# Attention's value products with hi and lo probabilities in one moving operand, part sums added by accumulating loads

## The chip, the cores and the metric

The kernel runs on one core of one Trainium2 chip. The metric is the device time of one execution in microseconds, as the median of several runs; lower is better. A core has TensorE (matmuls, with its weight loads), VectorE, ScalarE, GpSimd, and SyncE, whose queue issues nearly all DMAs of this kernel.

## What is computed

One layer over 1024 tokens of width 1024, in float32:

```python
h = rmsnorm(x, g_mix_pre)
proj = h @ w_in                      # q, k, v and forget logits of 8 heads, q, k, v of 8 more
y_fox = forgetting_attention(...)    # softmax(q.k/8 + c[t] - c[s]) v, causal; c = cumsum(log sigmoid(f))
y_chk = chunked_relpos_attention(...)  # softmax(q.k/8 + bias) v, own and 8 previous chunks of 64
x = x + rmsnorm(concat(rmsnorm(y_fox), rmsnorm(y_chk)) @ w_out)
x = x + rmsnorm(memory_cross_attention(rmsnorm(x), rmsnorm(mem)))   # 4 heads, 256 memory tokens
x = x + rmsnorm(square(relu(rmsnorm(x) @ w_ff1)) @ w_ff2)           # hidden 4096
```

Heads have 64 columns. A tolerance close to float32 is wanted, so the kernel splits each factor into a hi and a lo part in the rounded matmul format (F32R) and multiplies hi·hi, hi·lo and lo·hi.

## The kernel before

**Stages.** First the inputs are normalised and the values of the first eight heads ("f") are projected (`value_part`, `values_out`). Then comes one long attention phase (`attention_phase`), in which the q, k and later v projections of 8 pairs of heads, the scores, the transposes of the probabilities, the value products, the keys and values of the memory and the first half of the output projection are interleaved. After it follow the second half of the output projection, the cross attention, and the two matrices of the MLP, each in an order written out by hand.

**Who sets the order in attention.** The order is not written out; a planner in the kernel makes it while the program is recorded. `Flow` keeps a clock of its own. Generators (`value_steps`, `turn_steps`, `score_steps`, `side_steps`, `rstd_steps`, `filler_steps`, in this order of preference) each offer the next step of TensorE with a cost in microseconds and a condition; the first whose condition holds is recorded. Work of other engines is put into lists for VectorE "V", ScalarE "S", GpSimd "G" and the DMA queue "D" with a cost (`flow.put`, `flow.chain`, `flow.load`) and is recorded when the clock reaches it. `Tokens` count free buffers of each kind. On the chip each engine then runs its own list in order; a step that comes sooner or later than planned doesn't change the order, it makes an engine wait.

**Value products.** For a head and a group of two query blocks of 128, `turn_steps` transposes the probabilities of two key blocks into one bank of PSUM (four squares of 128; at an edge of the mask one of them is dead and left out, and the slots are turned so that it is the first or the last). ScalarE copies the bank to a hi tile `ph` (L582), VectorE makes the lo tile `pl` (L579). `value_steps` then multiplies (L613): the stationary operand is a tile of 128 keys by 128 columns, 64 of the values' hi part and 64 of their lo part. It is loaded for each matmul. Four matmuls make a step: (first key block, ph), (second, ph), (second, pl), (first, pl), each over the one or two live query blocks, all summed in one tile `pv`. Its partitions 0 to 63 hold hi values times (hi + lo) probabilities, 64 to 127 the lo values'. When a group's steps are through, ScalarE copies `pv` to `ot` (L622) and two DMAs store the two halves of partitions to DRAM tensors `od…h` and `od…l` (L628).

**Head outputs.** `Outputs.one` later loads both parts of a block of 128 rows by 512 tokens (L929), adds them (L920; GpSimd for the first half of the heads, VectorE for the second), splits the sum into hi and lo (L921, L922), squares it (L924) and sums the squares (L899). `rstd_steps` sums them over partitions by matmuls `ssh` (L942), and a GpSimd power (L950) gives the factor that `mix_steps` applies to the output projection.

**Gates.** `side_steps` transposes the log-forget gates by eight matmuls `ftr` (L401) when the planner's clock has passed 10; ScalarE copies them out, a VectorE scan (L409) sums them along the tokens, and the sums go by way of DRAM (`cd`) to the bias tiles of the "f" heads. Its three tiles `ea`, `la`, `ua` use three of the four `klo` buffers, which otherwise hold the lo part of the keys.

**Buffers.** The large tiles come from a pool `u4` of 34 buffers of 4 KB a partition. PSUM has two banks each of four kinds: `mm` (projections), `s` (scores), `tr` (transposes) and `pv`.

Of the kernel before, what the change touches and what calls it, by code (L numbers as in the profile page):

```python
# [14 lines left out]
F32 = mybir.dt.float32  # L15
F32R = mybir.dt.float32r
# [6 lines left out]
P = 128  # L23
# [112 lines left out]
def build(ctx, tc, nc, out, t):  # L136
# [16 lines left out]
    def u4(name, shape, dt=F32R):  # L153

        return up.tile(list(shape), dt, tag="u4", bufs=34, name=name)
# [44 lines left out]
    od = [[[dr.tile([P, HT], F32, name=f"od{k}_{h}{m}") for m in "hl"] for h in range(2)] for k in range(KC)]  # L200
# [18 lines left out]
    def bias_rows(part):  # L219

        if part == 0:
# [14 lines left out]
            dict(s=2, tr=2, pv=2, mm=2, sp=5, p=2, klo=4, bias=2, raw=2, w=2, ot=3, u4=6,  # L236
# [139 lines left out]
    def forget_gates():  # L376

        z, e, l, u = [p1.tile([P, TB, 8], F32, tag="fg", bufs=4, name=f"f{n}") for n in "zelu"]
        ea, la, ua = [p1.tile([8, S], F32, tag="klo", bufs=4, name=f"f{n}a") for n in "elu"]
# [27 lines left out]
        def scan():  # L407
            vec.memset(ua, 0.0)
            vec.tensor_tensor_scan(la, ea, ua, 0.0, op0=ALU.add, op1=ALU.add)  # L409
# [146 lines left out]
    def turn_steps():  # L556
        for n, a, g in units:
            for c, (kbs, slots, dead) in enumerate(key_steps(n, g)):
# [8 lines left out]
                ph = p1.tile([P, 4, P], F32R, tag="ph", bufs=2, name=f"ph{nm}")  # L567
                pl = p1.tile([P, 4, P], F32R, tag="pl", bufs=2, name=f"pl{nm}")
# [15 lines left out]
                trs[n, a, g, c] = ph, pl  # L584
# [3 lines left out]
    def value_steps():  # L588
        landed = [all_of(("od", k), 32) for k in range(2)]
        for n, a, g in units:  # L590
# [4 lines left out]
            for c, (kbs, slots, dead) in enumerate(steps):  # L595
                yield (0.48, lambda: there(("t", n, a, g, c), ("v", n, 0), ("v", n, 1))
                       and (c or free["pv"].ready() and free["ot"].ready()))
                if c == 0:
                    free["pv"].take()
                    pv = mm_tile([P, 2, P], f"pv{n}{a}{g}", "pv")  # L600
                ph, pl = trs.pop((n, a, g, c))
                full = 1 if dead == [0] else 0
                todo = [(full, ph), (1 - full, ph), (1 - full, pl), (full, pl)]
                for m, (half, x) in enumerate(todo):
# [3 lines left out]
                    else:  # L608
# [4 lines left out]
                    nc.tensor.matmul(pv[:, q0:q0 + k1 - k0, :], v, x[:, k0:k1, :], start=c == 0 and m == 0,  # L613
                                     stop=c + 1 == len(steps) and m == 3, skip_group_check=True)
                free["p"].give(flow.end)

            def leave(pv=pv, kind=kind, nm=f"{n}{a}{g}", a=a, kcol=kcol, g=g, step=1 if kind == "f" else -1):
                box = {}

                def copy():  # L620
                    box["t"] = p1.tile([P, 2, P], F32, tag="ot", bufs=3, name=f"ot{nm}")
                    nc.scalar.activation(box["t"][:, :, ::step], pv, AF.Copy)  # L622

                def store(at):
                    free["pv"].give(at)
                    done = all_of(("ot", nm), 2, lambda end: (free["ot"].give(end), landed["fc".index(kind)](end)))
                    for m in range(2):
                        flow.load(at, lambda m=m: nc.sync.dma_start(  # L628
                            od[kcol][g // 2][m][a * 64:a * 64 + 64, (g % 2) * 256:(g % 2) * 256 + 256],
# [1558 lines left out]
```

## Time and profile before

| | |
|---|---|
| runs of the kernel before | 1488.75 us median of 3 (1487.15 to 1489.96) |
| the profiled execution | 1486.78 us, of which the span of the core's instructions is 1485.0 |
| TensorE busy | 1462.4 us, 98% |
| VectorE, ScalarE, GpSimd busy | 927.7, 796.4, 378.1 us |
| DMA | 239.5 MB, 161 GB/s on average |

The busy shares say which engine is full over the whole span; a share of a stretch of 100 us says it for a stage. A row of a group gives the number of instructions, the sum and the mean of their durations and the idle time ahead of them. A row of the timeline gives start and duration of instructions that follow each other, and in brackets the idle time of the engine ahead of them and what ended it. Durations of neighbouring matmuls overlap, so that the distance between starts is the better measure of what one costs. Times in the timeline count from the start of the span. The stretches list, for each window, busy time of TensorE, its weight loads, VectorE, ScalarE and GpSimd, each with its number of instructions, then the granted TensorE clock (1.00 is full speed), the share of the DMA engines and their GB/s.

### The profile page before, as it was taken

To read this page: it belongs to the slowest core of one execution; us is meant where nothing else is said; L and a number is where in the kernel's file an instruction comes from. 1 tells how busy PE (TensorE), PEld (TensorE's weight loads), DVE (VectorE), ACT (ScalarE), POOL (GpSimd) and SP (SyncE) were. 2 spreads that over 40 slices of the span, in tenths; PEclk is the share of its full clock that TensorE was granted. 3 is DMA by queue.
4 is the path that set the end of the run, shared out by engine and by line. 5 is a ranking of instruction groups with operands and counts; after the bars stand their busy time and mean duration, and the time that the engine had idled before them with its cause. 6 is when DMAs were issued, how large, how long until landed. Compare 5 with 4: busy or idle time off the path is not lost. (4 is left out here: it accounts for less than half of the span.)

```text
span 1485.0 us, 21433 instructions
## 1 busy us (share of the span) xinstructions
PE 1462.4 (98%) x7564; PEld 1245.2 (84%) x7564; DVE 927.7 (62%) x1599; ACT 796.4 (54%) x1426; POOL 378.1 (25%) x464
## 2 busy tenths in 40 slices
PE   8899999999999999999999999999999999999998
PEld 7788888888889988888888887888888888888886
DVE  4857666466465654974374587675555665656577
ACT  7647666576566663563354454545555553443542
POOL 1334344335244310421031423432233000000021
PEclk9999999999999999999999999999999999999999
DMA  8033323424225568451241446764444685435475
GB/s 327 29 94 108 93 65 98 148 69 137 83 73 153 186 244 305 153 202 57 91 164 58 140 159 228 240 241 151 154 156 171 243 345 184 142 137 203 176 249 198
DMA packets 95355, 239.54 MB, mean 161 GB/s; under 512 B 11896, under 2 KB 20224, under 8 KB 95248
## 3 DMA queue, kind: packets, MB, share of 16 engines
q1 hardware_dynamic: 95248, 238.18, 46.8%
q8 instruction: 59, 0.97, 0.3%
q14 instruction: 48, 0.39, 0.1%
HBM read 170.45 MB, written 59.30 MB: 155 GB/s over the span
## 5 line engine op out<-in xcount | busy, mean ns | idle before, releaser
L579 DVE TENSOR_TENSOR pl<-ptr,ph 128x512 fp32r<-128x512 f32 (+1 forms) x152 | 92.4, 616 | 63.5 <-ACT ph L582 63.0
L582 ACT ACTIVATE ph<-ptr 128x512 fp32r<-128x512 f32 (+1 forms) x152 | 79.8, 540 | 48.5 <-PE ptr L573 45.9
L1912 ACT ACTIVATE whif<-ra 128x1024 fp32r<-128x1024 f32 x37 | 39.3, 1062 | 122.3 <-PE fy L175 62.6
L1914 DVE TENSOR_TENSOR wlof<-ra,whif 128x1024 fp32r<-128x1024 f32 x37 | 45.3, 1225 | 91.2 <-ACT whif L1912 91.1
L2028 POOL TENSOR_SCALAR rf<-sf 128x1 f32<-128x1 f32 x8 | 8.3, 1032 | 325.4 <-ACT jf L2013 325.1
L176 PE MATMUL fx<-vhif,wlof 128*128 128x512 f32 x168 | 65.4, 389 | 0.0
L175 PE MATMUL fx<-vlof,whif 128*128 128x512 f32 x168 | 65.4, 389 | 0.0
L174 PE MATMUL fx<-vhif,whif 128*128 128x512 f32 x168 | 65.4, 389 | 0.0
L613 PE MATMUL pv<-pl,vs 128*128 128x256 f32 (+1 forms) x304 | 64.6, 294 | 0.2 <-DVE pl L579 0.2
L613 PEld LDWEIGHTS pv<-ph,vs 128*128 128x128 f32 x304 | 53.1, 189 | 7.3
L613 PE MATMUL pv<-ph,vs 128*128 128x256 f32 (+1 forms) x304 | 58.1, 272 | 0.0
L1802 POOL TENSOR_TENSOR sc<-wf,wf 128x512 f32<-128x512 f32 x14 | 21.3, 1522 | 143.5 <-DMA wf<-in_w_ff 113.2
L174 PE MATMUL k<-hT_hi,whik 128*128 128x512 f32 x128 | 52.6, 411 | 0.0
L174 PE MATMUL q<-hT_hi,whiq 128*128 128x512 f32 x128 | 51.1, 399 | 1.3 <-DVE qs L703 1.3
L174 PE MATMUL mq<-h2T_hi,whimq 128*128 128x512 f32 x128 | 51.6, 403 | 0.0
L174 PE MATMUL yw<-whiwo,yT_hi 128*128 128x512 f32 x128 | 50.6, 396 | 0.4 <-ACT yt L1065 0.4
L174 PE MATMUL ym<-whimo,oT_hi 128*128 128x512 f32 x128 | 50.3, 394 | 0.1
L176 PE MATMUL k<-hT_hi,wlok 128*128 128x512 f32 x128 | 50.3, 393 | 0.0
L175 PE MATMUL k<-hT_lo,whik 128*128 128x512 f32 x128 | 50.3, 393 | 0.0
L176 PE MATMUL q<-hT_hi,wloq 128*128 128x512 f32 x128 | 50.1, 392 | 0.1
L175 PE MATMUL q<-hT_lo,whiq 128*128 128x512 f32 x128 | 50.1, 392 | 0.0
L175 PE MATMUL mq<-h2T_lo,whimq 128*128 128x512 f32 x128 | 50.0, 391 | 0.0
(597 smaller groups left out, 4979.7 us busy)
## 6 DMA issues: line engine op xcount, KB each, us to landing
ra<-gd SPq DMA_DIRECT2D x56, 512.0 KB, 3.5
wg<-in_w_ff SPq DMA_DIRECT2D x56, 512.0 KB, 4.9
wf<-in_w_ff SPq DMA_DIRECT2D x38, 512.0 KB, 3.9
gd<-s SPq DMA_DIRECT2D x48, 256.0 KB, 2.1
wrawmq<-in_w_mq SPq DMA_DIRECT2D x16, 512.0 KB, 3.8
wrawmo<-in_w_mo SPq DMA_DIRECT2D x16, 512.0 KB, 3.7
gd<-u SPq DMA_DIRECT2D x32, 256.0 KB, 2.1
gd<-g SPq DMA_DIRECT2D x25, 256.0 KB, 2.2
```

Of the source, the lines that this page charges most:

```text
L174: nc.tensor.matmul(ps, lh, rh, start=start, stop=False, skip_group_check=more)
L175: nc.tensor.matmul(ps, lh, rl, start=False, stop=False, skip_group_check=more)
L176: nc.tensor.matmul(ps, ll, rh, start=False, stop=stop, skip_group_check=more)
L579: flow.put("V", at, 0.56 if dead else 0.7, lambda: nc.vector.tensor_sub(pl[:, live, :], tr[:, live, :], f(ph[:, live, :])), done)
L582: flow.put("S", flow.end, 0.49 if dead else 0.6, lambda ph=ph, tr=tr, live=live: nc.scalar.activation(ph[:, live, :], tr[:, live, :], AF.C ...
L613: nc.tensor.matmul(pv[:, q0:q0 + k1 - k0, :], v, x[:, k0:k1, :], start=c == 0 and m == 0, stop=c + 1 == len(steps) and m == 3, skip_group_ ...
L1802: eng.tensor_sub(sc[:, k1], r0[:, k0], r1[:, k0])
L1912: nc.scalar.activation(ah, ra, AF.Copy)
L1914: nc.vector.tensor_sub(al, ra, f(ah))
L2028: nc.gpsimd.tensor_scalar(r, ssf[b][:, 0:1], ssf[b][:, 1:2], EPS, op0=ALU.add, op1=ALU.add)
```

## The change

Four things are edited together.

1. **One moving operand.** `ph` and `pl` become the halves of one tile `both`. A step is two matmuls instead of four; each sends the hi and the lo probabilities of one key block through one load of the values, as up to 512 columns. `pv` now has separate sums for hi and for lo probabilities, 512 columns, a whole bank.
2. **Three parts, added by loads.** `ot` and its copy are twice as wide. Two DMAs store three parts: hi·hi and hi·lo (partitions 0 to 63, both sums) and lo·hi (64 to 127, the first sum); lo·lo, which was summed before, is dropped. `Outputs.one` loads part 0 from SyncE's queue and adds parts 1 and 2 by two DMAs on GpSimd's queue that accumulate into the loaded tile, one after the other. The adds on GpSimd and VectorE go, and so do the tiles `oil`.
3. **Gates.** The sum of gates uses the two `bias` buffers instead of three of `klo`; its scan takes a minimum with its own input in place of an add of zeros, so that the memset goes. The transposes of the gates wait until the planner's clock has passed 13 instead of 10.
4. **Buffers.** `u4` has 32 buffers instead of 34 (the planner starts with 8 free tokens instead of 6), the room goes to the wider `ot` and to 4096 bytes of scratch for DMAs from GpSimd (256 before); the tile `rt` moves to the tag `ot`. The planner's costs follow: a value step 0.35 or 0.46 instead of 0.48, the copy 0.6 instead of 0.4, an accumulate 0.9 on GpSimd and 4.5 until it has landed.

```diff
-        return up.tile(list(shape), dt, tag="u4", bufs=34, name=name)
+        return up.tile(list(shape), dt, tag="u4", bufs=32, name=name)
...
-        ea, la, ua = [p1.tile([8, S], F32, tag="klo", bufs=4, name=f"f{n}a") for n in "elu"]
+        ea, la = [p1.tile([8, S], F32, tag="bias", bufs=2, name=f"f{n}a") for n in "el"]
...
-            vec.memset(ua, 0.0)
-            vec.tensor_tensor_scan(la, ea, ua, 0.0, op0=ALU.add, op1=ALU.add)
+            vec.tensor_tensor_scan(la, ea, ea, 0.0, op0=ALU.add, op1=ALU.min)
...
-                todo = [(full, ph), (1 - full, ph), (1 - full, pl), (full, pl)]
-                for m, (half, x) in enumerate(todo):
+                for m, half in enumerate((full, 1 - full)):
...
-                    nc.tensor.matmul(pv[:, q0:q0 + k1 - k0, :], v, x[:, k0:k1, :], start=c == 0 and m == 0,
-                                     stop=c + 1 == len(steps) and m == 3, skip_group_check=True)
+                    nc.tensor.matmul(pv[:, :, q0 * P:(q0 + k1 - k0) * P], v, x[:, :, k0:k1, :].rearrange("p m k q -> p m (k q)"),
+                                     start=c == 0 and m == 0, stop=c + 1 == len(steps) and m == 1, skip_group_check=True)
...
-        yield 0.87, lambda: flow.now > 10.0 and free["tr"].ready(2)
+        yield 0.87, lambda: flow.now > 13.0 and free["tr"].ready(2)
...
-                            (eng, add_cost, lambda: adder.tensor_add(o, o, low)),
...
-                    for m, x in enumerate((o, low)):
-                        flow.load(flow.now, lambda x=x, kc=kc, m=m: nc.sync.dma_start(x, od[kc][th][m]), here, 3.0)
+                    def add(at, m=1, o=o, src=od[kc][th], loaded=loaded):
+                        if m == 3:
+                            return loaded(at)
+                        flow.put("G", at, 0.9, lambda: nc.gpsimd.dma_start(o, src[m], accum_op=ALU.add),
+                                 lambda end: add(end + 4.5, m + 1, o, src, loaded), 1)
+
+                    flow.load(flow.now, lambda o=o, src=od[kc][th]: nc.sync.dma_start(o, src[0]), add, 3.0)
```

Three places of the program's order. The first is on TensorE at the start of attention: `k` and `q` are the projections of the first pair of heads, `q_1…` (here q_1_943, then q_1_915) the second half of the queries, `ftr` the gates' transposes. Before:

```order
L176 MATMUL k_0_890<-hT_hi_200,wlok_804 128x512
L174 MATMUL k_0_890<-hT_hi_201,whik_803 128x512
L175 MATMUL k_0_890<-hT_lo_205,whik_803 128x512
L176 MATMUL k_0_890<-hT_hi_201,wlok_804 128x512
L401 MATMUL ftr_925<-ident,fe 8x128 x4
L401 MATMUL ftr_930<-ident,fe 8x128 x4
L174 MATMUL k_0_890<-hT_hi_201,whik_803 128x512
L175 MATMUL k_0_890<-hT_lo_205,whik_803 128x512
L176 MATMUL k_0_890<-hT_hi_201,wlok_804 128x512
L174 MATMUL q_1_943<-hT_hi_206,whiq_798 128x512
```

And now, at the same place:

```order
L176 MATMUL k_0_873<-hT_hi_185,wlok_787 128x512
L174 MATMUL q_1_915<-hT_hi_190,whiq_781 128x512
L175 MATMUL q_1_915<-hT_lo_194,whiq_781 128x512
L176 MATMUL q_1_915<-hT_hi_190,wloq_782 128x512
L174 MATMUL q_1_915<-hT_hi_190,whiq_781 128x512
L175 MATMUL q_1_915<-hT_lo_194,whiq_781 128x512
L176 MATMUL q_1_915<-hT_hi_190,wloq_782 128x512
L174 MATMUL q_1_915<-hT_hi_191,whiq_781 128x512
L175 MATMUL q_1_915<-hT_lo_195,whiq_781 128x512
L176 MATMUL q_1_915<-hT_hi_191,wloq_782 128x512
L401 MATMUL ftr_932<-ident,fe 8x128 x4
L401 MATMUL ftr_937<-ident,fe 8x128 x4
```

The transposes have moved behind the last k matmuls and behind nine of the q half.

The second place is on TensorE as well, in the first head's first group: two full value steps and one with a dead square (`vs` are values, a row with "x2" two equal instructions). Before:

```order
L613 MATMUL pv_1198<-ph_1163,vs_0_190 128x256 x2
L613 MATMUL pv_1198<-pl_1164,vs_0_190 128x256 x2
...
L613 MATMUL pv_1198<-ph_1232,vs_3_193 128x256
L613 MATMUL pv_1198<-ph_1232,vs_3_193 128x128
L613 MATMUL pv_1198<-pl_1233,vs_3_193 128x128
L613 MATMUL pv_1198<-pl_1233,vs_3_193 128x256
```

Now:

```order
L611 MATMUL pv_1178<-p_1145,vs_0_174 128x512 x2
L611 MATMUL pv_1178<-p_1152,vs_1_175 128x512 x2
...
L611 MATMUL pv_1178<-p_1207,vs_3_177 128x512
L611 MATMUL pv_1178<-p_1207,vs_3_177 128x2x128
```

Two matmuls with 512 columns stand for four with 256, and 512 and twice 128 for 256, 128, 128 and 256.

The third is GpSimd's queue at the second and third group of head outputs (`oin` are the loaded tiles, `rs` the power behind the sum of squares `ssh`). Before, the only rows of `oin` there are the two adds of the second group:

```order
L920 TENSOR_TENSOR oin_6620<-oin_6620,oil_6622 128x512 x2
L920 TENSOR_TENSOR oin_6621<-oin_6621,oil_6623 128x512 x2
```

Now the accumulates of the second group end (first four rows), and those of the third and fourth follow:

```order
L924 DMA oin_6120<-od_1_88 128x512
L924 DMA oin_6120<-od_1_90 128x512
L924 DMA oin_6121<-od_1_92 128x512
L924 DMA oin_6121<-od_1_94 128x512
L924 DMA oin_6300<-od_0_95 128x512
L924 DMA oin_6300<-od_0_97 128x512
L924 DMA oin_6301<-od_0_99 128x512
L924 DMA oin_6301<-od_0_101 128x512
L948 TENSOR_TENSOR rs_6361<-rs_6361,mhalf 128x4
L924 DMA oin_6300<-od_0_95 128x512
L924 DMA oin_6300<-od_0_97 128x512
L924 DMA oin_6301<-od_0_99 128x512
```

The second accumulates of the third group stand behind the power `rs`, which waits for `ssh`. On TensorE 57 output matmuls (`yw`) stood between the end of the memory's keys (`mk`) and `ssh` of the second group before, and 87 now.

More of the change, by code (lines that the diff above doesn't have):

```diff
@@ L198, in build @@
     rall = const.tile([P, TB], F32, name="rall")
[L200 removed]
+    od = [[dr.tile([3, P, HT], F32, name=f"od{k}_{h}") for h in range(2)] for k in range(KC)]
     yd = [dr.tile([P, D], F32, name=f"yd{b}") for b in range(TB)]
@@ L883, in pump @@
                 self.left.pop(0)
-                for _ in range(9):
+                for _ in range(7):
                     free["u4"].take()
@@ L892, in one @@
             os = [u4(f"oin{th}{g}{i}", (P, 2, HT), F32) for i in range(2)]
-            ol = [u4(f"oil{th}{g}{i}", (P, 2, HT), F32) for i in range(2)]
-            eng, add_cost, adder = ("G", 1.45, nc.gpsimd) if g == 0 else ("V", 0.7, nc.vector)
             parts[th, g] = yh, yl, sq
@@ L903, in done @@
                     seen["sq", th, g] = end
-                    for _ in range(4):
+                    for _ in range(2):
                         free["u4"].give(end)
```

39 lines of the change are left out of this document (19 added, 20 removed).

## The prediction

> **What bounds the kernel now.** I read the page first, for the busy shares, then the list of what TensorE waited for, then the stretches.
>
> ```profile
> PE 1462.4 (98%) x7564; PEld 1245.2 (84%) x7564; DVE 927.7 (62%) x1599; ACT 796.4 (54%) x1426; POOL 378.1 (25%) x464
> PE v L174 <- ACT hT_hi L1380: 6.1, 2, 5.2
> PE ftr L401 <- DVE vs L1437: 3.4, 1, 3.4
> PE tr_h3T L1114 <- DVE ym L1010: 1.5, 1, 1.5
> PE q L174 <- DVE qs L703: 1.3, 1, 1.3
> 300.00:400.00 100.00, 99.91 (x611) 88.77 (x610) 61.28 (x182) 65.80 (x144) 41.67 (x55) 1.00 0.31 93
> ```
>
> TensorE is busy for 1462 of 1485 us, and in the attention phase for 99.9 of 100 us. No single wait is over 6 us. So time can only come from TensorE's own stream of instructions, and it is lost wherever that stream starts to wait. Since matmuls overlap, the mean time of one says little; what counts is the distance from one start to the next, read from the timeline.
>
> **Part 1: the value matmuls (L613).** This is how many there are, by shape, and what a step of them takes:
>
> ```profile
> L613 PE MATMUL pv<-pl,vs 128*128 128x256 f32 x224 | 55.6, 300 | 0.0
> L613 PE MATMUL pv<-pl,vs 128*128 128x128 f32 x80 | 22.2, 277 | 0.2 <-DVE pl L579 0.2
> 129.96 0.40 PE L176 MATMUL q<-hT_hi,wloq 128*128 128x512 f32 x1
> 130.20 0.28 PE L500 MATMUL sf1g<-kd,qs 128*128 128x256 f32 x1
> 130.32 0.28 PE L501 MATMUL sf1g<-kl,qs 128*128 128x256 f32 x1
> 130.44 0.40 PE L613 MATMUL pv<-ph,vs 128*128 128x256 f32 x2
> 130.67 0.40 PE L613 MATMUL pv<-pl,vs 128*128 128x256 f32 x2
> 130.91 0.28 PE L500 MATMUL sf1g<-kd,qs 128*128 128x256 f32 x1
> ...
> 132.28 0.34 PE L613 MATMUL pv<-ph,vs 128*128 128x256 f32 x2
> 132.46 0.44 PE L613 MATMUL pv<-pl,vs 128*128 128x128 f32 x2
> 132.74 0.39 PE L174 MATMUL q<-hT_hi,whiq 128*128 128x512 f32 x1
> ...
> 301.13 0.33 PE L500 MATMUL sc0g<-kd,qs 128*128 128x384 f32 x1
> 301.30 0.34 PE L501 MATMUL sc0g<-kl,qs 128*128 128x384 f32 x1
> ```
>
> Half of the matmuls are listed (pl; the ph half is the same), so 304 of each kind and 608 in all, four to a step: 152 steps. A step at an edge of the mask has one short half (128 columns), and there are 80 of those; 72 are full. A matmul with 512 columns takes 0.23 to 0.24 us to the next start (129.96 to 130.20), one with 384 takes 0.17 (301.13 to 301.30), one with 256 takes 0.12: the cost goes by columns. A full step takes 130.91 - 130.44 = 0.47 us, which is four times 0.12. A step with a short half takes 132.74 - 132.28 = 0.46 us, though it has 768 columns instead of 1024, which at this rate would be 0.35. It is therefore not bound by its columns but by something that counts matmuls: each brings its own weight load, and 0.46 / 4 = 0.115 us each is what four loads would need one after the other, since a 128-column matmul is too short to hide the next load.
>
> The change sends hi and lo probabilities through one weight load. A full step becomes two matmuls of 512: 2 x 0.23 = 0.46 us, against 0.47: 72 x 0.01 = 0.7 us. A short step becomes 512 and 256 columns: 0.23 + 0.12 = 0.35 us, against 0.46, and both are long enough to hide a load of 0.115: 80 x 0.11 = 8.8 us. Together **9.5 us less**, all of it on TensorE's path. No row shows a moving operand of two separate runs. If its second run cost as much as a matmul of its own, nothing would be gained; at the other end, full steps that follow transposes may save a little more, and I put the most at 12.5. I take 9.5, since columns set the cost in all rows whose loads are hidden.
>
> Each step's copy out of PSUM (L622) doubles to 128x512, on ScalarE:
>
> ```profile
> L622 ACT ACTIVATE ot<-pv x64: 362/384/387, 111.0 to 515.7; 128x256 f32<-128x256 f32 x64
> L924 ACT ACTIVATE oin<-oin x12: 613/621/637, 349.4 to 544.9; 128x512 f32<-128x512 f32 x12
> L579 DVE TENSOR_TENSOR pl<-ptr,ph 128x512 fp32r<-128x512 f32 (+1 forms) x152 | 92.4, 616 | 63.5 <-ACT ph L582 63.0
> wg<-in_w_ff SPq DMA_DIRECT2D x56, 512.0 KB, 4.9
> ```
>
> That is 64 x (0.62 - 0.38) = 15 us more over 400 us in which ScalarE is 66% busy; it becomes 70%, and I cost it at nothing. If the cover were gone it would be at most those 15 us. The first matmul of a step now needs the lo half as well as the hi half; the planner waited for both anyway, so this costs nothing, and uncovered it would be up to one VectorE split (0.62 us) for a step. Two u4 buffers fewer, of which the planner now counts two more as free, I cost at nothing: in the program's order a u4 buffer is written again no sooner than 69 instructions after its last use (94 before), some 7 us at 9 instructions to a microsecond, and the weights of the last stage (4.9 us to land) are fetched four steps of 24 matmuls ahead, 22 us. Uncovered it would be a few microseconds for each late load.
>
> **Part 2: the gate sums, later.** At the start of attention, rows of TensorE and then of the engines that it waits for:
>
> ```profile
> 67.01 0.39 PE L176 MATMUL k<-hT_hi,wlok 128*128 128x512 f32 x1
> 70.77 1.86 PE L401 MATMUL ftr<-ident,fe 128*8 128x128 f32 x8 [3.37 <-DVE vs L1437]
> 72.28 0.77 PE L174 MATMUL k<-hT_hi,whik 128*128 128x512 f32 x1
> 75.17 0.47 PE L174 MATMUL q<-hT_hi,whiq 128*128 128x512 f32 x1 [1.26 <-DVE qs L703]
> 72.20 1.39 DVE L228 COPY rrow<-rrow 8x511 f32<-8x511 f32 x1
> 73.61 1.41 DVE L703 SCALAR_TENSOR_TENSOR qs<-q,qs 64x512 fp32r<-64x512 f32 x2
> 76.91 2.28 DVE L409 TENSOR_TENSOR_SCAN fla<-fea,fua 8x1024 f32<-8x1024 f32 x1
> 86.08 0.29 POOL L462 TENSOR_SCALAR_AFFINE_SELECT biasf<-biasf 128x128 f32<-128x128 f32 x1 [10.13 <-DMA biasf<-cd]
> 92.25 0.39 PE L500 MATMUL sf0g<-kd,qs 128*128 128x512 f32 x1
> 70.70:72.20 1.50, 1.43 (x7) 0.88 (x8) 1.47 (x6) 1.49 (x3) 1.46 (x2) 0.50 0.00 0
> 74.00:76.00 2.00, 0.83 (x4) 0.74 (x5) 1.78 (x4) 1.24 (x3) 1.95 (x2) 1.00 0.73 246
> ```
>
> The second query half (q, from 75.17) can't start before VectorE has emptied the bank of the first, at 75.0. In the meantime the kernel before does the eight gate transposes (ftr) and three k matmuls for free. In the changed order three k matmuls and then nine of the q half stand ahead of ftr. VectorE's rows up to L703 are the same, so q still starts at 75.15; TensorE now runs out of k matmuls at about 67.9 (67.01 and four times 0.23) and idles in one piece of 7.2 us, and ftr is paid after it: 8 x 0.11 = 0.9 us. The granted clock fell to 0.50 after the idle piece of 3.4 us, and was 1.00 again some 3 us after work resumed. Before, that slow time was spent on ftr and k, which nobody waited for. Now it falls on q: 3.3 us (70.7 to 74.0) at half speed lose 1.7. Sum: **2.6 us more**, between 0.9 (no penalty of the clock) and 3.6 (slow for longer); below nothing it can't be, as q is held by the same VectorE row. The sum of gates ends some 5 us later (76.91 + 2.28 before; the 0.91 of its memset goes), so the masked bias comes at about 91 instead of 86.4, and the scores that need it start at about 95: still covered, by 3 to 4 us. If that cover were gone, scores would wait by the difference.
>
> **Part 3: the parts are added by loads.** Before: two loads for each of 16 row blocks and an add on GpSimd or VectorE. Now: one load and two accumulating DMAs from GpSimd's queue, the second behind a wait for the first. No accumulating DMA and no DMA from GpSimd is in the trace. The nearest rows:
>
> ```profile
> L920 POOL TENSOR_TENSOR oin<-oin,oil x8: 1285/1294/1681, 343.4 to 517.1; 128x512 f32<-128x512 f32 x8
> L929 SPq DMA_DIRECT2D oin<-od_1h x8: 377/422/645, 504.5 to 533.8; - x8
> DMA to landing us min/median/max: 2.7/5.0/7.1
> 519.89 2.28 DVE L899 TENSOR_TENSOR sq<-sq,oin 128x512 f32<-128x512 f32 x3
> 522.51 0.95 PE L942 MATMUL ssh<-o,sq 128*128 128x1 f32 x8
> ```
>
> One accumulate, issue and landing, is between 0.38 + 2.7 = 3.1 us and 1.68 + 7.1 = 8.8 us (a whole GpSimd instruction for its issue); the middle is 0.42 + 5.0 = 5.4. The place that decides is the sum of squares ssh of the second block group (522.51): its sq was ready at 522.2, so there is no margin to speak of. The chain becomes longer by two accumulates, less the add of 1.3, less 1.7 because four loads instead of eight stand in one burst (4 x 0.42). In the changed order 30 more output matmuls stand between the end of the memory keys, which starts the chain, and ssh: 30 x 0.23 = 6.9 us. So ssh is late by 2a - 9.9 us, with a the time of one accumulate: nothing up to a = 4.95, 0.9 at 5.4, 7.7 at 8.8. It counts twice: behind ssh hangs a GpSimd power, and behind that, in its queue, the next group's second accumulates. I take a = 5.4 and, for two late groups with 0.3 of margin, **1.5 us more**. For the first of the four groups I cost nothing: behind its last accumulates on GpSimd stand softmax scalings, which have about as long to spare; if not, it would be a further 1 to 3 us.
>
> The Trainium skill, DMA: Bandwidth & Descriptors, section "Anatomy of one DMA — SWDGE (gpsimd) path", fits 2.0 us and bytes at 436 GB/s to one such DMA; for 256 KB my estimate from it is 2.6 us. By that rule ssh would never wait, and the sum would be 1.5 us lower. The plain loads above took 5.0 in the middle, so the trace speaks against it where DMAs come in bursts, and I leave the sum as it is.
>
> **Sum.** -9.5 + 2.6 + 1.5 = -5.4 us. The profiled execution took 1486.78 us (span 1485.0), so such a one would take 1481.4. The median of the runs is 1488.75, 2.0 above it; for a median I forecast 1483.4.
>
> **Rivals.** (1) The accumulates land in time and the clock recovers at once: -9.5 (to -12.5) + 0.9, thus 1476 to 1480. For it: the middle row is only 0.45 us from the point at which ssh waits. Against it: the granted 0.50 after a shorter idle piece.
> (2) Slower: the accumulates are late. At a = 8.8 both groups wait 7.7 us, 15.4 together: -9.5 + 2.6 + 15.4 = +8.5, thus 1497. It decides from a = 6.65, where 2 x 3.4 us eat the gain of 6.9. For it: landings of up to 7.1 us are in the trace; GpSimd's queue is in order, and softmax scalings stand behind the waits. Against: half of all landings were under 5.0.
> The Trainium skill, same page, section "SWDGE vs HWDGE vs iDMA", says that GpSimd writes such a DMA's descriptors into SBUF, from which VectorE's two-port mode locks it out; no run here shows that yet. It would push a up and speaks for this rival.
> (3) The change doesn't do what it says: the joined operand streams no faster than two matmuls. Then +2.6 + 1.5 = +4.1, thus 1492.9. For it: no such operand is in the trace. Against: 512, 384 and 256 columns cost by columns alone.
>
> **How the numbers follow.** The forecast (1480 to 1487) has 0.50, rival 1 0.17, rival 2 0.20, rival 3 0.13. A measurement here can tell about 0.2%, 3 us. Faster: 0.43 of the forecast's 0.50, all of rival 1, and 0.02 of rival 2 near its point: 0.62. Same: 0.07, 0.06 of rival 2 and 0.03 of rival 3: 0.16. Slower: 0.12 and 0.10: 0.22. The range goes from 1476 (rival 1's end) to 1494 (rival 3 and the milder half of rival 2); what is left out is about 0.15.
>
> **What would show it.** Right, if 304 value matmuls fewer are there and a short step takes 0.35 us; if TensorE idles about 7 us ahead of q and the clock is 0.50 after it; if ssh waits 0 to 2 us on sq. Wrong, if a short step stays at 0.46, if an accumulate takes over 6.65 us, or if ScalarE's larger copies make TensorE wait for a pv bank, of which there are two.

## The result, and the profile after

The changed kernel took 1496.47 us in the median of 4 runs (1495.48 to 1498.36), the kernel before 1488.53 (1487.15 to 1489.96) beside it: a ratio of 1.0055, with a 95% interval of 1.0037 to 1.0072. It is **8 us slower**. I had forecast 1483.4 and a range that ended at 1494, so the forecast was wrong in its sign.

The page of the changed kernel, with the lines that answer to those of before (busy times; queues with packets, MB and share of the DMA engines; groups; DMA issues):

```profile
PE 1460.3 (98%) x7260; PEld 1229.4 (82%) x7260; DVE 923.1 (62%) x1590; ACT 804.8 (54%) x1426; POOL 395.4 (26%) x488
...
q0 software_dynamic: 4608, 8.39, 3.2%
...
L620 ACT ACTIVATE ot<-pv 128x512 f32<-128x512 f32 x64 | 38.0, 593 | 25.2 <-PE pv L611 24.3
...
oin<-od POOLq DMA_DIRECT2D x32, 256.0 KB, 7.4
```

The 304 matmuls fewer are there (7564 to 7260). PE's busy time, though, is only 2 us lower, while the value matmuls alone gave up 10.8 us from start to start: other matmuls take longer, those at half clock among them. The queue q0 is new: GpSimd's DMAs, which land 7.4 us after their issue. The list of what TensorE waited for shows two new heads:

```profile
PE yw L174 <- ACT yt L1063: 7.5, 6, 2.2
PE q L174 <- DVE qs L702: 7.0, 1, 7.0
...
PE ptr L572 <- POOL spc0g L515: 1.3, 1, 1.3
...
PE ptr L572 <- DMA oin<-od: 0.7, 1, 0.7
PE ssh L940 <- DVE sq L896: 0.4, 1, 0.4
```

The wait for q is the one that the gate part was to bring. The wait of the output matmuls (yw) for ScalarE's copies yt is the surprise, and ssh, where I had looked for the loss, hardly waits. The stretches tell where in time that is; first the changed kernel, then the kernel before (columns as in the prediction: busy time of PE, PEld, DVE, ACT and POOL, then granted clock, DMA share and GB/s):

```profile
75.00:100.00 25.00, 24.69 (x101) 19.39 (x102) 9.86 (x15) 5.17 (x9) 1.80 (x4) 0.90 0.45 124
300.00:400.00 100.00, 98.01 (x542) 83.78 (x541) 61.48 (x180) 68.43 (x145) 43.65 (x59) 1.00 0.45 112
499.00:565.00 66.00, 58.09 (x250) 45.89 (x249) 26.34 (x39) 34.19 (x56) 25.08 (x28) 0.92 1.02 254
```

```profile
499.00:565.00 66.00, 65.59 (x342) 55.82 (x341) 35.85 (x52) 39.10 (x63) 10.73 (x9) 1.00 0.73 252
```

Between 499 and 565 us, the output stage, TensorE is busy for 58.1 us instead of 65.6, its granted clock is 0.92, and it takes 250 matmuls instead of 342 (up to 505 us the kernel before is still in the attention phase, with its short matmuls). The DMA engines are busy throughout (1.02 against 0.73; a share over 1 says that packets overlap) and yet move no more bytes by the profile's count (254 against 252 GB/s).

By the starts of TensorE's instructions, the changed kernel stands like this against the kernel before: +3.9 us at the first masked scores (96.1 against 92.3), -6.3 at the last matmul of the memory keys (498.9 against 505.2), +8.2 at the last of the output stage's memory values (586.3 against 578.1), and +9.5 at the end. So the attention phase does gain, 10.2 us from the first masked scores on, and the 87 us behind it lose 14.5.

How the wait for yt comes about is to be read from three engines at one place: ScalarE first, then TensorE, then GpSimd.

```profile
546.96 0.72 ACT L915 ACTIVATE yT_hi<-oin,gcol 128x512 fp32r<-128x512 f32 x1 [2.18 <-DMA oin<-od]
547.59 0.61 ACT L918 ACTIVATE oin<-oin 128x512 f32<-128x512 f32 x1
548.11 0.67 ACT L1063 ACTIVATE yt<-yw,rs 128x512 f32<-128x512 f32 x1
...
554.16 0.72 ACT L915 ACTIVATE yT_hi<-oin,gcol 128x512 fp32r<-128x512 f32 x1 [3.91 <-DMA oin<-od]
554.78 0.67 ACT L1063 ACTIVATE yt<-yw,rs 128x512 f32<-128x512 f32 x1
```

```profile
548.83 0.50 PE L174 MATMUL yw<-whiwo,yT_hi 128*128 128x512 f32 x1 [0.99 <-ACT yt L1063]
552.25 1.02 PE L940 MATMUL ssh<-o,sq 128*128 128x1 f32 x8 [0.41 <-DVE sq L896]
555.50 0.80 PE L174 MATMUL yw<-whiwo,yT_hi 128*128 128x512 f32 x1 [2.23 <-ACT yt L1063]
```

```profile
549.24 0.86 POOL L924 DMA_DIRECT2D oin<-od  x1 [2.62 <-DMA oin<-od]
```

GpSimd's row shows how such loads come late: it issues one 2.62 us late, since the accumulate before it on the same row block hadn't landed. ScalarE stands still for 3.91 us, waiting for another load of this last block group, issued at 545.75 and landed at 554.13. The copy yt that would empty a bank of yw is the next row in its queue, and TensorE starts again 0.05 us after that copy ends (554.78 + 0.67 = 555.45). So the row block that is late isn't the one that TensorE waits for; it holds up the queue in which the copy stands. The Trainium skill, Perfetto Trace Analysis, section "Tensor Engine Instruction (MATMUL, LD_WEIGHTS)", calls these queues strict FIFO on ScalarE, VectorE and GpSimd; the rows agree.

### The profile page after: what moved, and what is told of

Same layout as the page of the kernel before. It is cut to its first block, busy times and chain, and to the rows that moved or that the text cites. A ratio compares the mean times of both kernels' runs of the same rounds, so it can differ in the third digit from the quotient of the medians.

```text
span 1494.4 us, 20838 instructions
## 1 busy us (share of the span) xinstructions
PE 1460.3 (98%) x7260; PEld 1229.4 (82%) x7260; DVE 923.1 (62%) x1590; ACT 804.8 (54%) x1426; POOL 395.4 (26%) x488
## 3 DMA queue, kind: packets, MB, share of 16 engines
q0 software_dynamic: 4608, 8.39, 3.2%
## 5 line engine op out<-in xcount | busy, mean ns | idle before, releaser
L578 DVE TENSOR_TENSOR p<-ptr,p 128x512 fp32r<-128x512 f32 (+1 forms) x152 | 92.1, 616 | 57.8 <-ACT p L581 56.8
L581 ACT ACTIVATE p<-ptr 128x512 fp32r<-128x512 f32 (+1 forms) x152 | 78.7, 539 | 44.1 <-PE ptr L572 43.4
L611 PE MATMUL pv<-p,vs 128*128 128x512 f32 (+1 forms) x304 | 85.8, 369 | 0.1
L611 PEld LDWEIGHTS pv<-p,vs 128*128 128x128 f32 x304 | 54.4, 188 | 10.4 <-DVE p L578 0.5
L175 PE MATMUL yw<-wlowo,yT_hi 128*128 128x512 f32 x128 | 51.6, 403 | 0.0
L176 PE MATMUL yw<-whiwo,yT_lo 128*128 128x512 f32 x128 | 51.6, 403 | 0.0
L620 ACT ACTIVATE ot<-pv 128x512 f32<-128x512 f32 x64 | 38.0, 593 | 25.2 <-PE pv L611 24.3
```

The lines of the kernel that those rows point to most:

```text
L175: nc.tensor.matmul(ps, lh, rl, start=False, stop=False, skip_group_check=more)
L176: nc.tensor.matmul(ps, ll, rh, start=False, stop=stop, skip_group_check=more)
L578: flow.put("V", at, 0.56 if dead else 0.7, lambda: nc.vector.tensor_sub(pl[:, live, :], tr[:, live, :], f(ph[:, live, :])), done)
L581: flow.put("S", flow.end, 0.49 if dead else 0.6, lambda ph=ph, tr=tr, live=live: nc.scalar.activation(ph[:, live, :], tr[:, live, :], AF.C ...
L611: nc.tensor.matmul(pv[:, :, q0 * P:(q0 + k1 - k0) * P], v, x[:, :, k0:k1, :].rearrange("p m k q -> p m (k q)"), start=c == 0 and m == 0, s ...
L620: nc.scalar.activation(box["t"][:, :, :, ::step], pv.rearrange("p m (k q) -> p m k q", q=P), AF.Copy)
```

## The experiments

All ratios are to the kernel before, run beside the kernel in question, with 95% intervals; in microseconds they are the ratio less 1, times 1489. The ratios come from all executions and can differ by about 1 us from what the medians give.

| kernel | median us | ratio (interval) | us |
|---|---|---|---|
| the changed kernel | 1496.47 | 1.0055 (1.0037 to 1.0072) | +8.2 |
| gate10 | 1494.44 | 1.0028 (1.0017 to 1.0038) | +4.2 |
| before_gates | 1491.71 | 1.0020 (1.0010 to 1.0030) | +3.0 |
| sum2 | 1486.29 | 0.9977 (0.9966 to 0.9988) | -3.4 |
| sum2_gate10 | 1483.17 | 0.9956 (0.9943 to 0.9969) | -6.6 |
| noacc | 1481.93 | 0.9957 (0.9942 to 0.9972) | -6.4 |
| acc1 | 1488.42 | 0.9991 (0.9980 to 1.0002) | -1.3 |
| plan7 | 1492.33 | 1.0021 (1.0012 to 1.0031) | +3.1 |
| before_acc1 | 1497.16 | 1.0054 (1.0041 to 1.0066) | +8.0 |
| before_noacc1 | 1490.94 | 1.0013 (1.0003 to 1.0024) | +1.9 |
| load3 | 1498.46 | 1.0064 (1.0051 to 1.0078) | +9.5 |
| pool_sum | 1481.36 | 0.9952 (0.9939 to 0.9964) | -7.1 |
| pool_sum2 | 1482.33 | 0.9949 (0.9936 to 0.9962) | -7.6 |

My theory after the result: accumulating loads land late, and with in-order queues this costs some 14 us of the output stage; the later gates cost 3 to 4; the joined operand gains what was forecast. The rivals: the new order of the work, the wider copies out of the banks or the fewer buffers cost the time; or what is moved by GpSimd's queue does, added or not.

### The gates: gate10 and before_gates

gate10 is the changed kernel with the earlier place of the transposes:

```diff
-        yield 0.87, lambda: flow.now > 13.0 and free["tr"].ready(2)
+        yield 0.87, lambda: flow.now > 10.0 and free["tr"].ready(2)
```

> The changed kernel with the gate transposes back at their earlier place (threshold 10 instead of 13). Theory (the later gates cost 2.6 to 3.9 us at the start, the accumulates the rest): about 1493.5 us, TensorE's idle of 7 us ahead of q gone, first masked scores 3 to 4 us earlier. Rival (the whole loss is in the output stage, and what the start loses is given back before it): 1496 as the changed kernel.

before_gates is the kernel before with the other side of it: threshold 13, the gate sums in bias tiles and the scan with one operand fewer.

> The kernel before with the change's gate part alone (sum of gates in bias tiles, threshold 13, one operand fewer in the scan). Theory: TensorE idles some 7 us ahead of q and runs at half clock after it, 2.6 to 3.9 us slower, about 1492 us. Rival (covered by later waits): 1488.5.

gate10 came to 1494.4, by the ratios 4.0 us under the changed kernel (2.0 by the two medians), with its first masked scores 3.2 us earlier (93.0 against 96.1), and before_gates to 3.0 us over the kernel before. The rows of TensorE in before_gates:

```profile
77.21 0.76 PE L174 MATMUL q<-hT_hi,whiq 128*128 128x512 f32 x1 [7.06 <-DVE qs L702]
80.84 1.03 PE L401 MATMUL ftr<-ident,fe 128*8 128x128 f32 x8
```

TensorE idles 7.06 us in one piece and the transposes follow. This part alone costs some 3 to 4 us, and nothing shows that any of it is given back.

### Without accumulating loads: sum2 and sum2_gate10

In sum2 the joined operand stays, and VectorE adds the two sums of a bank on the way out; two parts are stored, loaded and added on engines as in the kernel before. sum2_gate10 has the earlier gates besides.

```diff
-                    nc.scalar.activation(box["t"][:, :, :, ::step], pv.rearrange("p m (k q) -> p m k q", q=P), AF.Copy)
+                    nc.scalar.activation(box["t"][:, :, ::step], pv[:, 0].rearrange("p (k q) -> p k q", q=P), AF.Copy)
+                def add():
+                    o = box["t"][0:64, :, ::step]
+                    nc.vector.tensor_add(o, o, pv[0:64, 1].rearrange("p (k q) -> p k q", q=P))
```

> The changed kernel with its joined operand and its later gates, but without accumulating loads: VectorE adds the two sums of a bank on the way out, and the two parts that are left are loaded and added on GpSimd and VectorE as in the kernel before. Theory (accumulates that land late cost 14 to 15 us): 1488.5 - 10.7 + 3.9, thus about 1482 us, and TensorE waits under 2 us for yw and ssh. Rival (the loss is that of the re-planned order and of the busier way out of the banks): stays at 1494 to 1497.

> The joined operand alone: VectorE adds the two sums on the way out, no accumulating loads, gates at their earlier place. Theory: the gain of the value matmuls in full, 1488.5 - 10.7, thus about 1478 us, faster than both kernels. Rival (the joined operand's gain is given back further on whatever the parts' path): 1488 to 1493.

sum2 took 1486.3 and sum2_gate10 1483.2: 10 to 12 us under the changed kernel and its gate10, and faster than the kernel before, but 4 and 5 us over what I expected. The output stage runs through; what TensorE waited for in sum2_gate10:

```profile
PE sc2g L499 <- DVE mnc2g L503: 1.5, 2, 1.3
...
PE yw L174 <- ACT yt L1067: 0.8, 1, 0.8
```

Waits for yw fell from 7.5 to 0.8 us. What is missing shows when the time from each start on TensorE to the next is summed by kind of work, from the first q matmul to the last of the memory values: against the kernel before, value matmuls -9.7, but scores +1.9, projections +2.6, transposes of probabilities +1.4 and yw +0.8. I put this down to VectorE's 64 adds, which stand in the way of the score reductions and splits that TensorE waits for; this is argued, and pool_sum below tests it.

### The adding or the queue: noacc

The same kernel, order, queue and bytes; GpSimd's loads overwrite instead of adding, so that the sum of the parts is left out.

```diff
-                        flow.put("G", at, 0.9, lambda: nc.gpsimd.dma_start(o, src[m], accum_op=ALU.add),
+                        flow.put("G", at, 0.9, lambda: nc.gpsimd.dma_start(o, src[m]),
```

> The changed kernel with GpSimd's loads as plain loads: they overwrite instead of adding, so the sum of the three parts is left out; same queue, bytes and order. If the adding is what makes them slow: they land in 3 to 5 us as the plain ones on SyncE's queue, the output stage loses under 5 us, and the time is 1486 to 1489. If it is GpSimd's queue or the crowd of transfers in that stretch: landing stays near 7 us and the time at 1494 to 1498.

1481.9 us, below even the 1486 to 1489 that I expected: 14.6 us less than the changed kernel, though the late gates are still in it. The rows of noacc: its queue, its issues on GpSimd, from issue to landing for the first block group (295 to 345 us, where the DMA engines are about half busy) and for the other three (495 to 560), and the output stage.

```profile
q0 software_dynamic: 2560, 8.39, 1.7%
...
L924 POOL DMA_DIRECT2D oin<-od x32: 536/538/757, 298.6 to 538.4; - x32
...
DMA to landing us min/median/max: 2.8/3.4/4.9
...
DMA to landing us min/median/max: 3.9/5.2/7.1
...
499.00:565.00 66.00, 65.42 (x306) 53.99 (x305) 29.89 (x41) 36.22 (x58) 16.56 (x28) 1.00 0.94 327
```

The same of the changed kernel:

```profile
L924 POOL DMA_DIRECT2D oin<-od x32: 865/878/1507, 299.2 to 552.9; - x32
...
DMA to landing us min/median/max: 5.4/6.3/7.5
...
DMA to landing us min/median/max: 4.2/7.8/9.4
```

Adding takes the median landing from 3.4 to 6.3 us where it is quiet and from 5.2 to 7.8 where it is crowded, and the issue on GpSimd from 0.54 to 0.88. The DMA engines' share for the same 8.39 MB goes from 1.7% to 3.2%: 32 loads took 0.032 x 16 x 1494.4 = 765 us of engine time, 23.9 each, against 0.017 x 16 x 1479.0 / 32 = 12.6. The accumulating loads also went in packets of 2 KB and the plain ones in packets of 4 KB, but the size of the packets isn't what costs: in the trace of the changed kernel an accumulating packet of 2 KB took 184 ns in the mean, a plain one of 2 KB on SyncE's queue 98 ns, and a plain one of 4 KB 190 ns. Without the adding the output stage runs at full clock, and the DMA engines move 327 GB/s there instead of 254. So it is the adding inside the transfer, and neither the queue nor the wider copies nor the new order of the work: those are all in noacc too.

The Trainium skill, Collectives: The Full Stack, section "Stop ④ — SDMA + CCE: where bytes move and the add happens", says of the add inside a collective's transfer that it is "read-read-write with the add free in between". Nearly twice the engine time agrees with a second read, though no row shows that read by itself; free it isn't here, since those engines are what the stage lacks.

### Half the dose: acc1

Two parts, of which GpSimd's accumulating load adds one; VectorE adds on the way out as in sum2.

```diff
-                        if m == 3:
+                        if m == 2:
                             return loaded(at)
```

> The changed kernel with one accumulating load for a row block instead of two: VectorE adds the two sums of a bank on the way out, so that two parts are stored, one loaded and one added by GpSimd's accumulating load. Theory (lateness is two accumulates of about 8 us, one behind the other): a single one fits into the time that there is, TensorE's waits for yw and ssh go from 13 us to under 4, and the time comes to that of the variant without accumulating loads, 1486 to 1488 us. Rival (the bytes that GpSimd's queue moves slow everything in that stretch): half of the loss stays, about 1491.

1488.4 us, 2.1 over sum2, its own pair without accumulates. Its row among TensorE's waits:

```profile
PE yw L174 <- ACT yt L1066: 4.3, 2, 3.7
```

The time is at the end of the theory's 1486 to 1488, and the waits are just over the 4 us that it allowed. By the ratios one accumulate of a block costs 2.1 us, hardly more than the intervals allow for, and two cost 14.6. That the cost is out of proportion isn't shown by this: in the one profile of each, from the last memory key to the last memory value, acc1 takes 4.3 us more than sum2 (77.9 against 73.6), and the changed kernel 12.2 more than noacc (87.4 against 75.2).

### The planner told the truth: plan7

```diff
-                                 lambda end: add(end + 4.5, m + 1, o, src, loaded), 1)
+                                 lambda end: add(end + 7.5, m + 1, o, src, loaded), 1)
```

> The changed kernel with one number of the planner changed: an accumulating load is taken to land after 7.5 us instead of 4.5, near the 7.2 measured. Theory (ScalarE's queue is in order, and yT_hi, put there too early, holds up the copies of yw that empty TensorE's banks): those waits of 7.5 us go, some come back as waits for y itself, 1489 to 1493 us. Rival (the sums come late whatever the order): 1495 to 1498.

1492.3 us, 5.1 under the changed kernel by the ratios, as expected of the theory. The waits for yw shrank from 7.5 to 4.5 us where I had them go, and some moved:

```profile
PE yw L174 <- ACT yt L1063: 4.5, 3, 1.9
PE ssh L940 <- DVE sq L896: 2.9, 2, 2.7
```

With yT_hi later in ScalarE's order, fewer copies yt stand behind it, and now ssh itself waits. A third of the 14.6 us was thus the order that goes with a wrong landing time; the rest stays, as it would if the sums are late whatever the order.

### One part of the change alone: before_acc1 and before_noacc1

The kernel before, with GpSimd's accumulating load in place of the second load and the engine's add (and one u4 buffer fewer, to make room for 4096 bytes of scratch for GpSimd's DMAs); before_noacc1 is the same without `accum_op`, so that the second part is left out of the sum.

> The kernel before with one part of the change alone: of the two parts of a row block the second is added by GpSimd's accumulating load instead of a load and an engine's add; matmuls and gates as before. Theory (one accumulate of about 8 us costs the output stage some 2 us, as between the two variants in which VectorE adds on the way out, with and without it): 1490 to 1492. Rival (the accumulates are late only where the joined operand and the planner's new order press that stage): 1488 to 1489 as the kernel before.

> The kernel before with one accumulating load for each row block, but as a plain load on GpSimd's queue that overwrites: the sum of the two parts is left out. Order, buffers and bytes are those of the kernel before with the accumulating loads alone (+8 us). If the adding inside the transfer makes the price: loads land in under 5.5 us and the time is 1487 to 1490. If it is the path of the sums over GpSimd's queue, or the one u4 buffer fewer: 1494 to 1497.

before_acc1 came to +8.0 us where I expected 1 to 3: a miss, and my theory's price of one accumulate from acc1 doesn't carry over. The rival fell too: accumulates are late here without a joined operand. before_noacc1 came to +1.9 us, just over the range that I gave it, so about 6 of the 8 us are the adding, and 2 the path over GpSimd or the buffer, which I didn't separate. The rows, of before_acc1 (its queue, what it issued, a wait, a stretch) and then of before_noacc1:

```profile
q0 software_dynamic: 2304, 4.20, 1.7%
...
oin<-od_1l POOLq DMA_DIRECT2D x8, 256.0 KB, 7.4
...
PE yw L174 <- ACT yt L1064: 2.4, 2, 2.2
...
499.00:592.00 93.00, 88.19 (x438) 73.30 (x437) 42.23 (x61) 47.92 (x75) 16.17 (x18) 0.98 0.82 245
```

```profile
q0 software_dynamic: 1280, 4.20, 0.8%
...
oin<-od_1l POOLq DMA_DIRECT2D x8, 256.0 KB, 4.7
...
499.00:592.00 93.00, 91.55 (x473) 77.51 (x473) 46.09 (x69) 52.01 (x83) 13.14 (x18) 1.00 0.75 254
```

Same order of instructions, same buffers, same bytes: the adding doubles the queue's share again and takes the landing from 4.7 to 7.4 us. From the last memory key to the last memory value before_acc1 took 6.7 us more than the kernel before, before_noacc1 1.1, in the one profile of each.

### Three loads and engine adds: load3

The parts stored as in the changed kernel, but loaded by SyncE (second and third in one load of 512 KB) and added on GpSimd and VectorE; gates at their earlier place.

> The joined operand with three parts stored as in the changed kernel, but no accumulating loads: SyncE loads all three parts (the second and third by one load of 512 KB) and GpSimd and VectorE add them, two adds for a row block; gates at their earlier place. Theory: nothing stands in the way out of the banks but ScalarE's wider copy, which costs nothing, so the gain of the value matmuls comes in full, 1478 us or 10.7 under the kernel before. Rival (16 more adds of 1.3 us on GpSimd and as many loads make the sums late as the accumulates did): 1484 to 1490.

1498.5 us, the slowest of all, and worse than even the rival had it. Most of it is one wait; TensorE, VectorE, ScalarE and GpSimd in turn:

```profile
354.25 0.69 PE L499 MATMUL sc2g<-kd,qs 128*128 128x384 f32 x1 [9.84 <-DVE mnc2g L503]
```

```profile
352.88 0.99 DVE L922 SCALAR_TENSOR_TENSOR yT_lo<-oin,gcol,yT_hi 128x512 fp32r<-128x512 f32 x1 [6.25 <-ACT yT_hi L921]
```

```profile
352.13 0.72 ACT L921 ACTIVATE yT_hi<-oin,gcol 128x512 fp32r<-128x512 f32 x1 [5.85 <-POOL oin L920]
```

```profile
346.92 1.26 POOL L919 TENSOR_TENSOR oin<-oin,oim 128x512 f32<-128x512 f32 x1 [15.28 <-DMA oim<-od]
349.61 1.26 POOL L919 TENSOR_TENSOR oin<-oin,oim 128x512 f32<-128x512 f32 x1 [1.43 <-DMA oim<-od]
350.83 1.26 POOL L920 TENSOR_TENSOR oin<-oin,oim 128x512 f32<-128x512 f32 x1
```

The first load of the first block group wasn't late: it was issued at 342.55 and landed 4.2 us later, and the planner has 4.0. But on GpSimd the second add of this row block (L920) stands behind the first add of the next one, which waited for its own load, 5.9 us from its issue, and each add takes 1.26 us. ScalarE waited for that second add, VectorE for ScalarE, and the score reduction that TensorE needed stood behind VectorE's yT_lo. After the wait the granted clock was at half for 10.2 us (349.6 to 359.8). It is the kind of chain that the changed kernel has, with plain loads and GpSimd's adds at its start and at another place. So the rival's ground, more adds and loads, fits these rows, at a higher price than I gave it; what the profiled execution loses behind the last memory value, 4.6 us against the kernel before, I can't place.

### A version that beats both: pool_sum and pool_sum2

ScalarE copies both sums at once (the change's wider copy), which frees the bank, and GpSimd adds them in SBUF before they are stored.

```diff
+                def add():
+                    o = box["t"][0:64]
+                    nc.gpsimd.tensor_add(o[:, 0], o[:, 0], o[:, 1])
-                flow.put("S", flow.end, 0.6, copy, store)
+                flow.put("S", flow.end, 0.6, copy, lambda at: (
+                    free["pv"].give(at), flow.put("G", at, 0.75, add, store, 1)))
```

> The joined operand without accumulating loads and with the gates at their earlier place, as the variant in which VectorE adds on the way out, but ScalarE copies both sums (128x512) and GpSimd adds them in SBUF, behind the bank's release; one u4 buffer fewer than before. Theory (the variant with VectorE gave 4.5 us of the gain back because its adds delay the score and split work that TensorE waits for): about 1479 us. Rival (the gain is given back in another way): 1483 as that variant; or GpSimd's scalings come later by up to 0.75 us each and TensorE waits for ptr: 1486 to 1490.

1481.4 us, 7.1 under the kernel before: better than sum2_gate10 by 0.6 us, which is within the intervals, and 2 us over the theory. So it isn't shown that VectorE's adds were what sum2 and sum2_gate10 gave back. Its waits:

```profile
PE pv L611 <- DVE p L578: 2.6, 2, 1.6
PE sc2g L499 <- DVE mnc2g L503: 1.7, 2, 1.5
```

pool_sum2 has two planner numbers nearer to what was measured:

```diff
-            eng, add_cost, adder = ("G", 1.45, nc.gpsimd) if g == 0 else ("V", 0.7, nc.vector)
+            eng, add_cost, adder = ("G", 2.5, nc.gpsimd) if g == 0 else ("V", 0.7, nc.vector)
-                        flow.load(flow.now, lambda x=x, kc=kc, m=m: nc.sync.dma_start(x, od[kc][th][m]), here, 3.0)
+                        flow.load(flow.now, lambda x=x, kc=kc, m=m: nc.sync.dma_start(x, od[kc][th][m]), here, 5.0)
```

> The variant in which GpSimd adds on the way out, with two of the planner's numbers nearer to what was measured: the add of a row block on GpSimd 2.5 us instead of 1.45, its loads landing after 5 us instead of 3. Theory (what is left of the loss there are VectorE's and ScalarE's in-order waits for row blocks that come later than planned: sc2g 1.7 and pv 2.6 us): about 1478. Rival (the waits have other grounds): 1481 as that variant.

The wait for sc2g is down to 0.4 us and that for pv to 1.0 us, yet the time, -7.6 us, can't be told from that of pool_sum: the 3 us of waits didn't come back as time. The starts of TensorE's work stand 1.5 us better from the first masked scores to the end in the one profile of each. That of pool_sum2 has the granted clock at half from 572.7 to 576.1, among the memory's values, where pool_sum has 1.00; by my estimate, from 0.43 us from start to start at half clock against 0.23, these 3.4 us lose 1.6. I can't place the rest.

## Why the prediction was wrong, step by step

**Part 1, the value matmuls: right.** I had 9.5 us. From start to start, the 72 full steps went from 35.3 to 34.3 us and the 80 short ones from 38.4 to 28.6, 10.8 together. A full step and a short one of the changed kernel:

```profile
129.77 0.62 PE L611 MATMUL pv<-p,vs 128*128 128x512 f32 x2
130.23 0.39 PE L174 MATMUL q<-hT_hi,whiq 128*128 128x512 f32 x1
...
136.31 0.51 PE L611 MATMUL pv<-p,vs 128*128 128x512 f32 x2
136.65 0.40 PE L174 MATMUL q<-hT_hi,whiq 128*128 128x512 f32 x1
```

130.23 - 129.77 = 0.46 and 136.65 - 136.31 = 0.34 us, where I had 0.46 and 0.35. The operand of two runs streams by its columns, and rival 3 is out. That the short steps were bound by their weight loads fits this, but isn't isolated: the joined step has fewer matmuls as well as fewer loads. The wider copies took 0.59 us each and cost nothing that can be seen, as forecast, nor did the two u4 buffers: noacc, which has both, stands at -6.4, and -10.8 + 3.5 for the gates is -7.3.

**Part 2, the gates: right in mechanism, short in size.** I had 2.6 us, bounds 0.9 to 3.6; the runs gave 3.0 (before_gates) and 4.0 (changed kernel against gate10). The idle piece was 7.03 us where I had 7.2. What I undersized was the clock: 3.3 us at half speed were forecast, and it lasted from 73.2 to 80.1, 5.0 us of it with work (from 75.1); in noacc, with the same gates, it lasted 10.2 us. The changed kernel's stretch is the first row; the other two belong to part 3:

```profile
73.20:80.10 6.90, 4.99 (x14) 3.58 (x15) 3.12 (x5) 0.70 (x2) 2.72 (x3) 0.51 0.73 196
...
520.40:523.80 3.40, 3.40 (x10) 2.63 (x9) 1.50 (x2) 2.03 (x4) 0.00 (x0) 0.50 1.09 291
554.50:561.30 6.80, 5.80 (x14) 4.55 (x15) 4.46 (x7) 6.67 (x11) 1.46 (x1) 0.50 1.03 277
```

**Part 3, the accumulates: the step that failed.** I costed one accumulate at 5.4 us, from plain loads on SyncE's queue, the middle between bounds of 3.1 and 8.8. In the groups that decide it took 7.8 us, past my own point of 6.65 from which the change is slower. The row that I took it from was of another kind of transfer: noacc's plain loads, 5.2 us, are what I had priced. (The 7.8 and the 5.2 include the issue, since time to landing counts from its start. My 5.4 had added the issue to a landing time that held it already; the row says 5.0.) What I took for an operation with the cost of a load keeps the DMA engines busy 1.9 times as long. Rival 2, late accumulates, is the case that came, and I had given it 0.20.

That its +8.5 us is so near the measured +8.2 is luck. At a = 7.8 my formula gives 2 x 5.7 = 11.4 us, where the changed kernel less noacc is 14.6, and the path was another one: I had TensorE wait for ssh, and ssh waited 0.4 us. So a sign that I had named for being right, ssh waiting 0 to 2 us, came true although the forecast failed. Between 499 and 565 us the waits for yw and ssh add up to 7.9 us (1.95, 0.46, 0.38, 1.50, 0.99, 0.41 and 2.23), and 9.2 us of work at half clock (the last two rows above) lose up to another 4.6. I had named what stands behind the waiting instructions on GpSimd, but not what stands behind them on ScalarE, and I had no term for the clock there. Why one accumulate costs 2 us in acc1 and 6 in before_acc1 isn't shown; their orders of work differ, and in the output stage of their profiles it is 4.3 and 5.6.

The first block group, costed at nothing or else 1 to 3 us, cost some 2: ptr waited 1.3 us for a softmax scaling on GpSimd and 0.7 for an accumulating load. noacc has 99.7 us of PE in 300 to 400 where the changed kernel has 98.0:

```profile
300.00:400.00 100.00, 99.72 (x551) 85.48 (x550) 61.15 (x181) 68.45 (x145) 40.29 (x58) 1.00 0.39 114
```

The two rules of the Trainium skill that I weighed, DMA: Bandwidth & Descriptors, section "Anatomy of one DMA — SWDGE (gpsimd) path": 2.0 us and the bytes at 436 GB/s, by my estimate 2.6 us for 256 KB, is just under the quickest plain load of noacc (2.8), and far from an accumulating one (6.3 where it was quiet). Section "SWDGE vs HWDGE vs iDMA", the lockout by VectorE: no run here was made to show it, and the longer issue with adding (0.88 against 0.54 in the middle, at least 0.87 against 0.54) was there throughout.

One slip of arithmetic: by its own terms the lower end of rival 1 is 1477, not 1476, which changes no chance.

In sum, against the kernel before: -10.8 (value matmuls), +3 to +4 (gates) and +14.6 (adding in the transfers) give +7 to +8; measured +8.2.

## What to carry to other kernels

Price an operation that no row shows by what it does, not by the row that looks most like it. A load that adds took 1.9 times the DMA engine time of a plain one, and where those engines were near full other transfers were later too: the stores of yt landed 6.8 us after their issue, against 4.4 in noacc. Where engines take their work in order, look behind each new wait on every engine that it passes through (here ScalarE), and not only at whoever needs the late data. A gain that saves TensorE's instructions needs a way out for the results that no TensorE wait hangs on: here the wide copy with an add in SBUF by the least busy engine kept 7 of the 10.8 us.

## What the runs showed of the hardware

- An accumulating load of 256 KB took 23.9 us of DMA engine time against 12.6 for a plain one from the same queue, 144 packets (4608 / 32; the data in 2 KB) against 80 (2560 / 32; in 4 KB), 0.88 us of GpSimd for its issue against 0.54, and landed 2.6 to 2.9 us later.
- The granted clock fell to half around idle pieces of TensorE of 1.95 us (ended at 520.0) and 2.23 us (ended at 555.5), and stayed there for 3.4 and 6.8 us; around those of 1.50 and 0.99 us (ended at 544.8 and 548.8) it stayed at 1.00. After the piece of 7.03 us it was at half for 5.0 us of work. Apart from the last one at each program's end, every stretch at half clock in the traces lasts 3.4, 6.8 or 10.2 us; at half clock matmuls of 512 columns start 0.43 us apart (520.74 to 521.17), at full clock 0.23.
